# A two-layer encoder trunk on one core: the first norm's factors by a shorter chain, and the first layer's sums queued behind them

## The chip, the cores and the metric

The kernel runs on 1 core of one Trainium2 chip. A core has five engines, each with its own instruction queue that it works through in order: TensorE (PE in the profile, with PEld for its weight loads), VectorE (DVE), ScalarE (ACT), GpSimd (POOL) and SyncE (SP). They wait for each other by semaphores. The metric is the device time of one execution in microseconds, lower is better.

## The reference

The input x has 512 positions of 1024 channels. Two layers follow each other. Each normalizes x, projects it by one wide matrix, runs three branches (a gated linear scan, a spatial gating, a windowed attention), merges them by gates, adds the result to x, and adds a squared-ReLU MLP of a second norm of x. A last norm ends the trunk. What the change touches is the norm and what is computed from it at once:

```python
def rms_norm(x, w):
    xf = x.astype(jnp.float32)
    y = xf * lax.rsqrt(jnp.mean(xf * xf, axis=-1, keepdims=True) + EPS)
    return (y * w.astype(jnp.float32)).astype(x.dtype)
...
for l in range(DEPTH):
    xn = rms_norm(x, ln1[l])
    z = xn @ w_in[l]   # split into the inputs of the branches and their gates
    ...
    x = x + merged @ w_out[l]
    hn = rms_norm(x, ln2[l])
    x = x + jnp.square(jax.nn.relu(hn @ w_up[l])) @ w_down[l]
return rms_norm(x, final_norm)
```

## The kernel before

**The norm's factor is applied late.** The kernel multiplies x by the norm's weights, projects that without waiting for the root, and multiplies each product by the factor of its row, rs = (mean of squares + eps)^-0.5, when it takes the product out of PSUM. So the projections can start before the factors are known, but no product leaves PSUM without them.

**How the factors come about.** For the first layer (`norm_feat`) ScalarE squares the eight pieces of x (four blocks of 128 rows, two halves each) with a running sum of each piece (L286, the tile ss). VectorE adds the halves (L291, tile s), then scales by 1/1024 and adds epsilon (L261, tile ms), and GpSimd raises that to the power -0.5 (L263, tile rs, 128 x 4). Both are traced with high priority. The other norms (`norm_tok`: the second norm of a layer, the first norm of the second layer, and the last norm in `finish`, L1084) go the same way. The norm of the scan's heads also uses `rstd_c`, but has one sum only. Three small operations of VectorE (L721 to L723, tile gsc) make half, minus half and minus one times the factors, for the products that need a sign or a half.

**Exact products in two parts.** Each float32 operand of a product is split: ScalarE rounds it to a high part (L196 for weights, L251 for activations, tiles wh and xs), VectorE subtracts to get the rest (L197 and L252, tiles wl and xs), and TensorE does three products of the parts. There are three tiles each for high and low weights.

**What runs first.** `project_bu` projects one branch's input by four weight chunks (products bu, L201 to L203); `norm_rows` then broadcasts rs over the partitions by TensorE (L270, product bc), ScalarE copies that to SBUF (L338, tile rb), and VectorE takes the four products out with it (L685). Next are three wide blocks of the projection. Each is done by the function `seven`, a scheme that replaces eight block products by seven: it needs sums and differences of the activations' blocks and of the weights' blocks.

- `left_x` makes the activation sums for four pairs of channel blocks (k = 0 to 3): in `left_sums` L369, L371, L372 and L375 (tile sf), then splits (L251, L252).
- `early_sums` makes weight sums in place: t1 = b11 + b12 (L392) and b12 + b22 (L394).
- `seven` makes b11 = t1 + b22 for product 6 (L420) and b21 + b11 for product 4 (L422), and splits each product's weights. The order of the first block is 1, 7, 6, 2, 5, 4, 3. Products 1 and 2 use activations as they are; products 7 and 6 need sums. Product 6 accumulates on the banks of product 1 (tA), which ScalarE must have read out with rs first (L732); product 7 (tC) needs banks that hold bu until L685.

In the profile, t is the first wide block (tA, tB, tC are its banks), g the other two. GELU of bu (L699 to L702) and the norm of the spatial gating (L813 to L819, with a power of one column at L818) are filled in between.

**What sets the order.** No order is written out by hand here. A planner simulates the program while it is built and fixes each engine's queue: it takes operations by priority when their inputs are ready by its own estimate. `high_priority` (and `hp()`, once `boost[0]` is set) raises the priority of what is traced inside. `tc.issue_after(ins)` puts every instruction that is traced in its block on ins's engine behind ins in that engine's queue; nothing else is made to wait.

At the start (L158, L159) one small square on ScalarE and one small power on GpSimd are run on constants.

Of the kernel before, what the change touches and what calls it, by code (L numbers as in the profile page):

```python
# [7 lines left out]
F32R = mybir.dt.float32r  # L8
U8 = mybir.dt.uint8
AF = mybir.ActivationFunctionType  # L10
# [4 lines left out]
D = 1024  # L15
# [44 lines left out]
def trunk(tc, xT, xt, ws, vec, fnb, bsb, snk, wst, rope, cmask, amask, ident, out):  # L60
# [49 lines left out]
    def SM(tag, w):  # L110
        return pad.tile([P, w], F32, tag="sm_" + tag, bufs=4 if tag == "lb" else NSM, name=nm(tag))
# [44 lines left out]
    nc.vector.memset(pad_t, 0.0)  # L156

    nc.scalar.activation(pad_t[:, 1:2], pad_t[:, 0:1], AF.Square)  # L158
    nc.gpsimd.tensor_tensor(pad_t[:, 2:3], onep_t, mhalf_t[:, 0:1], ALU.pow)  # L159

    def ln_ap(which, l, kt):
        c = {"ln1": 0, "ln2": 16, "fn": 32}[which] + (l * 8 if which != "fn" else 0) + kt
# [95 lines left out]
    def rstd_c(pt, n):  # L258
# [4 lines left out]
        nc.gpsimd.tensor_tensor(r, t, mhalf_t[:, 0:w], ALU.pow)  # L263
        return r

    def bcast(c):

        pt = PT("s", "bc")
        for j in range(4):
            nc.tensor.matmul(pt[:, j * P:(j + 1) * P], ap_of(c, j, [[0, P]]), id_t, start=True, stop=True)  # L270
        return pt
# [4 lines left out]
    def norm_feat(l, xf, xrows):  # L276

        n = Norm()
        n.xs, n.xf = [], xf
        for k in range(KT):  # L280
            hi, lo = T("x", "xh", F32R), T("x", "xl", F32R)
            split(xf[k], hi, lo, ln_ap("ln1", l, k))
            n.xs.append((hi, lo))
        ss = SM("ss8", 8)
        for j, x in enumerate(xrows):
            nc.scalar.activation(T("jk", "jk"), x, AF.Square, accum_out=ss[:, j:j + 1])  # L286
        for k in range(KT):
            nc.scalar.activation(xf[k], xf[k], AF.Copy, scale=ln_ap("ln1", l, k))
        s = SM("s4", 4)
        with tc.high_priority():  # L290
            nc.vector.tensor_tensor(s, ap_of(ss, 0, [[2, 4]]), ap_of(ss, 1, [[2, 4]]), ALU.add)  # L291
            n.rc = rstd_c(s, D)
        return n

    def norm_tok(which, l, xr, keep):

        n = Norm()
        n.xs, n.xf = [None] * KT, [None] * KT
        n.ss = SM("ss8", 8)

        def add(t, fl):
            j = T("jk", "jk")
            nc.scalar.activation(j, xr[t][fl], AF.Square, accum_out=n.ss[:, t * 2 + fl:t * 2 + fl + 1])

        def turn(fl, ts, banks="ss"):

            w = len(ts) * P
            c0 = ts[0] * P
            for d in range(4 * fl, 4 * fl + 4):
                if n.xs[d] is None:  # L310
                    n.xs[d] = (T("x", "xh", F32R), T("x", "xl", F32R))
                    if keep:
                        n.xf[d] = T("z" if d < 4 else "l", "xf")
                pt = PT(banks[d % 2], "xT")
                for i, t in enumerate(ts):
                    nc.tensor.transpose(pt[:, i * P:(i + 1) * P], xr[t][fl][:, (d % 4) * P:(d % 4 + 1) * P], id_t)
                src = pt[:, 0:w]
                parts = [x[:, c0:c0 + w] for x in n.xs[d]]
                if keep:
                    xf = n.xf[d][:, c0:c0 + w]  # L320
                    nc.scalar.activation(xf, src, AF.Copy, scale=ln_ap(which, l, d))
                    split(xf, *parts)
                else:
                    split(src, *parts, ln_ap(which, l, d))

        def end():
            s = SM("s4", 4)
            nc.vector.tensor_tensor(s, ap_of(n.ss, 0, [[2, 4]]), ap_of(n.ss, 1, [[2, 4]]), ALU.add)
            n.rc = rstd_c(s, D)

        n.add, n.turn, n.end = add, turn, end
        return n

# [43 lines left out]
        split(sb_.rearrange("p a b -> p (a b)"), *b_)  # L377
        h.update({5: two(a_, 0), 6: two(a_, 1), 7: two(b_, 0), 3: two(b_, 1)})

    def left_x(n):  # L380

        res = []
        for k in range(4):
            h = {1: two(n.xs[k], 0), 2: two(n.xs[k + 4], 0), 4: two(n.xs[k + 4], 1)}
            left_sums(lambda: T("xs", "xs", F32R), h, n.xf[k], n.xf[k + 4])
            res.append(h)
        return res

    def early_sums(raw):
        b11, b12, b22, b21, t1 = raw  # L390
        for i in range(2):
            nc.vector.tensor_tensor(t1[i], b11[i], b12[i], ALU.add)  # L392
        for i in range(2):
            nc.vector.tensor_tensor(b12[i], b12[i], b22[i], ALU.add)  # L394

    def seven(raw, hs, name, on, order=(1, 2, 6, 7, 5, 4, 3), between=None, apart=False):

        b11, t3, b22, b21, t1 = raw
        V = nc.vector

        banks = {}
        use = {1: ("c", b11, "P1"), 2: ("m", b21, "P2"), 6: ("c", b11, "P16"), 7: ("a", t3, "P7"),
               5: ("c", t1, "P165"), 4: ("a", b21, "P74"), 3: ("c", b22, "P1653")}

        def mms(pt, p, k, xh, xl, hi, lo, c, start):
            t = slice(p * P, (p + 1) * P)
            nc.tensor.matmul(pt, xh[:, t], hi[:, c], start=start and k == 0, stop=False, skip_group_check=True)  # L407
            nc.tensor.matmul(pt, xl[:, t], hi[:, c], start=False, stop=False, skip_group_check=True)  # L408
            nc.tensor.matmul(pt, xh[:, t], lo[:, c], start=False, stop=k == 3, skip_group_check=True)  # L409

        for n in order:
            tag, w, which = use[n]
            start = n in (1, 2, 7)
            if start:
                banks[tag] = [PT(tag, name + {"c": "A", "m": "B", "a": "C"}[tag]) for _ in range(2)]
            pts = banks[tag]
            with hp():
                for i in range(2):
                    if n == 6:
                        V.tensor_tensor(b11[i], t1[i], b22[i], ALU.add)  # L420
                    elif n == 4:
                        V.tensor_tensor(b21[i], b21[i], b11[i], ALU.add)  # L422
# [256 lines left out]
    for l in range(DEPTH):  # L679
# [31 lines left out]
        if l == 0:  # L711
            bu = project_bu()

        hx = left_x(n1)
        if l == 0:
            raw = uload(l, "un", 0)
            early_sums(raw)
            boost[0] = True
        rc = n1.rc
        sc = SM("gsc", 12)  # L720
        nc.vector.tensor_scalar(sc[:, 0:4], rc, 0.5, None, ALU.mult)  # L721
        nc.vector.tensor_scalar(sc[:, 4:8], rc, -0.5, None, ALU.mult)
        nc.vector.tensor_scalar(sc[:, 8:12], rc, -1.0, None, ALU.mult)  # L723
        vt = [None] * 4
        bv = [None] * 4

# [45 lines left out]
        for u in range(3):  # L772
            nxt = uload(l, "un", u + 1) if u < 2 else None
            if u == 0:
                seven(raw, hx, "t", on_tok, (1, 7, 6, 2, 5, 4, 3), (lambda: bu.extend(project_bu())) if l else None)
            else:
                seven(raw, hx, "g", on_gate(u - 1))
            if nxt:
                early_sums(nxt)
            raw = nxt  # L780
# [299 lines left out]
        def finish(ts):  # L1080

            n = len(ts)
            ss = SM("s4", 4)[:, 0:n]
            nc.vector.tensor_tensor(ss, ap_of(n1.ss, 2 * ts[0], [[2, n]]), ap_of(n1.ss, 2 * ts[0] + 1, [[2, n]]), ALU.add)  # L1084
            rc = rstd_c(ss, D)
# [185 lines left out]
```

## Time and profile before

| what | value |
|---|---|
| median of 3 runs | 1714.54 us |
| lowest and highest | 1712.42 and 1716.99 us |
| the profiled execution | 1714.73 us |
| its span, first to last instruction | 1712.9 us |
| mean granted TensorE clock | 0.994 |
| instructions | 22985 |
| data moved by DMA | 199.85 MB, mean 117 GB/s |

All rows quoted further down are from the profiled execution. Its times are microseconds from the start of the span. A row of a timeline gives start and duration, engine, line of the kernel, operation, output and inputs by the program's names with their shape, how many such instructions are merged, and in brackets how long the engine had been idle and what ended that. A tile's buffer numbers are left out, so all sums of activations are called sf. The granted clock is the share of TensorE's full speed that the chip allowed in a stretch.

### The profile page before, as it was taken

What the parts mean: (1) busy time and instruction counts of PE and PEld (TensorE: products, weight loads), DVE (VectorE), ACT (ScalarE), POOL (GpSimd) and SP (SyncE); (2) the same over time, 40 slices, a digit from 0 to 9 for tenths busy, and PEclk for the clock granted to TensorE, in tenths of its full rate; (3) what the DMA queues carried; (4) which work ended last, traced back from release to release, by engine and by line L of the source; (5) the groups of instructions that cost most, each with busy time, mean ns of one, the idle gap of its engine ahead of it and who ended that gap; (6) DMA issues with size and microseconds to landing.
All of it is one profiled execution on the core that took longest, in us unless ns stands there. A gap on an engine that the chain in (4) does not pass through costs nothing.

```text
span 1712.9 us, 22985 instructions
## 1 busy us (share of the span) xinstructions
PE 1675.5 (98%) x8536; PEld 1379.8 (81%) x8536; DVE 1285.7 (75%) x2049; ACT 1009.5 (59%) x1691; POOL 122.0 (7%) x198
## 2 busy tenths in 40 slices
PE   7999999999999999999999999999999999999997
PEld 5788887887778888888878888888877788888886
DVE  7896987678465758687889869876875567676877
ACT  6565578677325645455666666877882355545464
POOL 1021000000320000000010210000004100000001
PEclk9999999999999999999999999999999999999999
DMA  8243222231465233332333332322216453232311
GB/s 318 77 148 108 87 87 87 87 105 56 156 237 184 88 122 98 100 111 99 123 123 98 136 106 84 105 87 87 98 44 248 158 185 99 99 112 85 124 61 50
DMA packets 58144, 199.85 MB, mean 117 GB/s; under 512 B 7888, under 2 KB 8144, under 8 KB 58032
## 3 DMA queue, kind: packets, MB, share of 16 engines
q1 hardware_dynamic: 44496, 154.46, 27.0%
q0 software_dynamic: 13248, 43.40, 6.9%
q8 instruction: 67, 1.10, 0.3%
q10 hardware_dynamic: 288, 0.52, 0.1%
q14 instruction: 45, 0.37, 0.1%
HBM read 177.38 MB, written 20.97 MB: 116 GB/s over the span
## 4 chain that ended last, share of the span: by engine, by line
PE 86%; ACT 5%; DVE 4%; DMA 2%; issue 1%; POOL 1%; SPq 0%; POOLq 0%; ACTq 0%; DVEq 0%
PE up L202 7%; PE up L201 7%; PE up L203 7%; PE dA L408 3%; PE dA L407 3%; PE dA L409 3%; PE po L948 2%; PE gA L407 2%; PE wo L244 2%; PE at L540 2%; PE dC L408 2%; PE dC L407 2%; PE dC L409 2%; PE gA L409 2%; PE gA L408 2%; PE wo L243 2%
## 5 line engine op out<-in xcount | busy, mean ns | idle before, releaser
L196 ACT CAST wh<-wq 128x1024 fp32r<-128x1024 f32 x196 | 206.3, 1052 | 213.5 <-PE dA L408 49.2
L196 ACT CAST wh<-wr 128x1024 fp32r<-128x1024 f32 x171 | 179.6, 1050 | 247.5 <-PE up L202 88.7
L197 DVE TENSOR_TENSOR wl<-wr,wh 128x1024 fp32r<-128x1024 f32 x171 | 208.8, 1221 | 154.2 <-ACT wh L196 153.3
L197 DVE TENSOR_TENSOR wl<-wq,wh 128x1024 fp32r<-128x1024 f32 x196 | 239.0, 1221 | 89.0 <-ACT wh L196 87.8
L202 PE MATMUL up<-xl,wh 128*128 128x512 f32 x512 | 199.1, 389 | 0.0
L203 PE MATMUL up<-xh,wl 128*128 128x512 f32 x512 | 199.0, 389 | 0.0
L201 PE MATMUL up<-xh,wh 128*128 128x512 f32 x512 | 198.6, 389 | 0.0
L201 PEld LDWEIGHTS up<-xh,wh 128*128 128x128 f32 x512 | 96.1, 188 | 20.1
L203 PEld LDWEIGHTS up<-xh,wl 128*128 128x128 f32 x512 | 96.1, 188 | 20.0
L202 PEld LDWEIGHTS up<-xl,wh 128*128 128x128 f32 x512 | 96.1, 188 | 19.7
L407 PE MATMUL dA<-wh,sh 128*128 128x512 f32 x256 | 99.7, 390 | 0.0
L408 PE MATMUL dA<-wh,sh 128*128 128x512 f32 x256 | 99.6, 389 | 0.0
L409 PE MATMUL dA<-wl,sh 128*128 128x512 f32 x256 | 92.6, 389 | 0.0
L580 DVE TENSOR_TENSOR ex<-ex 128x512 f32<-128x512 f32 x112 | 74.8, 685 | 4.7 <-ACT kt L556 4.2
L407 PEld LDWEIGHTS dA<-wh,sh 128*128 128x128 f32 x256 | 48.0, 188 | 10.0
L409 PEld LDWEIGHTS dA<-wl,sh 128*128 128x128 f32 x256 | 48.1, 188 | 10.0
L408 PEld LDWEIGHTS dA<-wh,sh 128*128 128x128 f32 x256 | 48.1, 188 | 9.9
L263 POOL TENSOR_TENSOR rs<-ms,mhalf_t 128x4 f32<-128x4 f32 (+2 forms) x15 | 18.5, 1233 | 493.6 <-DVE ms L261 484.3
L554 DVE TENSOR_TENSOR qt<-qt,q 128x512 f32<-128x512 f32 x56 | 38.4, 686 | 18.9 <-ACT qt L553 18.5
L553 ACT ACTIVATE qt<-ex 128x512 f32<-128x512 f32 x56 | 37.7, 674 | 24.5 <-DVE ex L580 19.4
L251 ACT CAST sh<-sf 128x512 fp32r<-128x512 f32 x64 | 39.6, 619 | 19.4 <-DVE sf L372 17.5
L201 PE MATMUL gz<-xh,wh 128*128 128x512 f32 x128 | 50.7, 396 | 0.0
(405 smaller groups left out, 4343.1 us busy)
## 6 DMA issues: line engine op xcount, KB each, us to landing
wr<-in_ws_dram SPq DMA_DIRECT2D x171, 512.0 KB, 3.4
wq<-in_ws_dram SPq DMA_DIRECT2D x112, 512.0 KB, 4.3
thd<-zt POOLq DMA_DIRECT2D x32, 256.0 KB, 2.5
th<-thd POOLq DMA_DIRECT2D x32, 256.0 KB, 3.4
mgd<-mg POOLq DMA_DIRECT2D x16, 256.0 KB, 2.6
mcd<-th POOLq DMA_DIRECT2D x16, 256.0 KB, 3.1
mC<-mcd POOLq DMA_DIRECT2D x16, 256.0 KB, 7.2
mB<-mgd POOLq DMA_DIRECT2D x16, 256.0 KB, 6.6
```

The lines of the kernel that those rows point to most:

```text
L196: nc.scalar.copy(hi, raw)
L197: nc.vector.tensor_tensor(lo, raw, hi.bitcast(F32), ALU.subtract)
L201: nc.tensor.matmul(pt, whi, xhi, start=first, stop=False)
L202: nc.tensor.matmul(pt, whi, xlo, start=False, stop=False)
L203: nc.tensor.matmul(pt, wlo, xhi, start=False, stop=last)
L251: nc.scalar.copy(hi, src)
L407: nc.tensor.matmul(pt, xh[:, t], hi[:, c], start=start and k == 0, stop=False, skip_group_check=True)
L408: nc.tensor.matmul(pt, xl[:, t], hi[:, c], start=False, stop=False, skip_group_check=True)
L409: nc.tensor.matmul(pt, xh[:, t], lo[:, c], start=False, stop=k == 3, skip_group_check=True)
L553: nc.scalar.activation(qt.rearrange(shp, b=nb, h=2), e_q, AF.Exp)
L554: nc.vector.tensor_tensor(qt, qt, q, ALU.mult)
L580: nc.vector.tensor_tensor(o_ap, o_ap, ap_of(ex, i_, [[istep, 2]] + z), ALU.add)
```

## The change

Each square is scaled by 1024^-0.5 before it is squared, so the running sums are already means; one operation (`rstd_d`) adds the two halves and epsilon. All RMS norms of x use it. The warm-up power at the start goes. In each layer the three factor operations are traced ahead of the activation sums and with high priority, and in the first layer the fourth pair's activation sums, the weight sums b12 + b22 and those of `seven`'s first block (L420, L422) are queued on VectorE behind the last of the three.

```diff
-    nc.gpsimd.tensor_tensor(pad_t[:, 2:3], onep_t, mhalf_t[:, 0:1], ALU.pow)
...
+    def rstd_d(ss, t0, w):
+
+        t = SM("ms", 4)[:, 0:w]
+        nc.vector.scalar_tensor_tensor(t, ap_of(ss, 2 * t0, [[2, w]]), EPS, ap_of(ss, 2 * t0 + 1, [[2, w]]), ALU.add, ALU.add)
+        r = SM("rs", 4)[:, 0:w]
+        nc.gpsimd.tensor_tensor(r, t, mhalf_t[:, 0:w], ALU.pow)
+        return r
...
-            nc.scalar.activation(T("jk", "jk"), x, AF.Square, accum_out=ss[:, j:j + 1])
+            nc.scalar.activation(T("jk", "jk"), x, AF.Square, scale=D ** -0.5, accum_out=ss[:, j:j + 1])
...
-        s = SM("s4", 4)
         with tc.high_priority():
-            nc.vector.tensor_tensor(s, ap_of(ss, 0, [[2, 4]]), ap_of(ss, 1, [[2, 4]]), ALU.add)
-            n.rc = rstd_c(s, D)
+            n.rc = rstd_d(ss, 0, 4)
...
+    def behind(mark):
+
+        return tc.issue_after(mark.ins) if mark else contextlib.nullcontext()
+
-    def left_x(n):
+    def left_x(n, mark=None):
...
-            left_sums(lambda: T("xs", "xs", F32R), h, n.xf[k], n.xf[k + 4])
+            with behind(mark if k == 3 else None):
+                left_sums(lambda: T("xs", "xs", F32R), h, n.xf[k], n.xf[k + 4])
...
-    def early_sums(raw):
+    def early_sums(raw, mark=None):
...
-        for i in range(2):
-            nc.vector.tensor_tensor(b12[i], b12[i], b22[i], ALU.add)
+        with behind(mark):
+            for i in range(2):
+                nc.vector.tensor_tensor(b12[i], b12[i], b22[i], ALU.add)
...
-            with hp():
+            with hp(), behind(mark):
                 for i in range(2):
                     if n == 6:
                         V.tensor_tensor(b11[i], t1[i], b22[i], ALU.add)
...
-        hx = left_x(n1)
+        rc = n1.rc
+        sc = SM("gsc", 12)
+        with tc.high_priority():
+            nc.vector.tensor_scalar(sc[:, 0:4], rc, 0.5, None, ALU.mult)
+            nc.vector.tensor_scalar(sc[:, 4:8], rc, -0.5, None, ALU.mult)
+            mark = nc.vector.tensor_scalar(sc[:, 8:12], rc, -1.0, None, ALU.mult)
+        hx = left_x(n1, mark if l == 0 else None)
         if l == 0:
             raw = uload(l, "un", 0)
-            early_sums(raw)
+            early_sums(raw, mark)
             boost[0] = True
-        rc = n1.rc
-        sc = SM("gsc", 12)
-        nc.vector.tensor_scalar(sc[:, 0:4], rc, 0.5, None, ALU.mult)
-        nc.vector.tensor_scalar(sc[:, 4:8], rc, -0.5, None, ALU.mult)
-        nc.vector.tensor_scalar(sc[:, 8:12], rc, -1.0, None, ALU.mult)
...
-                seven(raw, hx, "t", on_tok, (1, 7, 6, 2, 5, 4, 3), (lambda: bu.extend(project_bu())) if l else None)
+                seven(raw, hx, "t", on_tok, (1, 7, 6, 2, 5, 4, 3), (lambda: bu.extend(project_bu())) if l else None, mark=None if l else mark)
```

The squares in `norm_tok` are scaled in the same way, and `end` there and `finish` (L1084) call `rstd_d` in place of the sum and `rstd_c`.

More of the change, by code (lines that the diff above doesn't have):

```diff
@@ L302, in add @@
             j = T("jk", "jk")
-            nc.scalar.activation(j, xr[t][fl], AF.Square, accum_out=n.ss[:, t * 2 + fl:t * 2 + fl + 1])
+            nc.scalar.activation(j, xr[t][fl], AF.Square, scale=D ** -0.5, accum_out=n.ss[:, t * 2 + fl:t * 2 + fl + 1])
         def turn(fl, ts, banks="ss"):
@@ L326, in end @@
         def end():
-            s = SM("s4", 4)
-            nc.vector.tensor_tensor(s, ap_of(n.ss, 0, [[2, 4]]), ap_of(n.ss, 1, [[2, 4]]), ALU.add)
-            n.rc = rstd_c(s, D)
+            n.rc = rstd_d(n.ss, 0, 4)
         n.add, n.turn, n.end = add, turn, end
@@ L392, in early_sums, with seven @@
             nc.vector.tensor_tensor(t1[i], b11[i], b12[i], ALU.add)
-        for i in range(2):
-            nc.vector.tensor_tensor(b12[i], b12[i], b22[i], ALU.add)
-    def seven(raw, hs, name, on, order=(1, 2, 6, 7, 5, 4, 3), between=None, apart=False):
+        with behind(mark):
+            for i in range(2):
+                nc.vector.tensor_tensor(b12[i], b12[i], b22[i], ALU.add)
+    def seven(raw, hs, name, on, order=(1, 2, 6, 7, 5, 4, 3), between=None, apart=False, mark=None):
         b11, t3, b22, b21, t1 = raw
@@ L1082, in finish @@
             n = len(ts)
-            ss = SM("s4", 4)[:, 0:n]
-            nc.vector.tensor_tensor(ss, ap_of(n1.ss, 2 * ts[0], [[2, n]]), ap_of(n1.ss, 2 * ts[0] + 1, [[2, n]]), ALU.add)
-            rc = rstd_c(ss, D)
+            rc = rstd_d(n1.ss, ts[0], n)
             for i, t in enumerate(ts):
```

## The prediction

> **What bounds the kernel now.** I read the page first. TensorE is busy nearly all the time, so only a stretch where it stands still or runs slowly can be worth anything.
>
> ```profile
> PE 1675.5 (98%) x8536; PEld 1379.8 (81%) x8536; DVE 1285.7 (75%) x2049; ACT 1009.5 (59%) x1691; POOL 122.0 (7%) x198
> ```
>
> Then the waits of TensorE alone (engine, line, what it waited for: us in total, times, longest).
>
> ```profile
> PE bu L201 <- ACT wh L251: 5.8, 1, 5.8
> PE bc L270 <- POOL rs L263: 5.2, 1, 5.2
> ```
>
> The first is the start of the program, which the change leaves alone. The second is the longest wait inside it: the broadcast of the first norm's factors (bc) waits for GpSimd's power, rs. The timeline shows how that wait comes about (start, duration, engine, line, operation; the bracket is the idle time before).
>
> ```profile
> 29.05 0.19 ACT L286 ACTIVATION_READ_ACCUMULATOR jk<-xt 128x1 f32 x1
> ...
> 31.90 0.15 DVE L291 TENSOR_TENSOR s<-ss 128x4 f32<-128x4 f32 x1
> 31.97 1.22 DVE L420 TENSOR_TENSOR wq<-wq,wq 128x1024 f32<-128x1024 f32 x1
> 33.11 1.22 DVE L394 TENSOR_TENSOR wq<-wq,wq 128x1024 f32<-128x1024 f32 x1
> ...
> 35.72 1.22 DVE L420 TENSOR_TENSOR wq<-wq,wq 128x1024 f32<-128x1024 f32 x1
> ...
> 36.85 0.16 DVE L261 TENSOR_SCALAR ms<-s 128x4 f32<-128x4 f32 x1
> 36.92 0.41 DVE L372 SCALAR_TENSOR_TENSOR sf<-sf,x 128x256 f32<-128x256 f32 x1
> 37.10 4.89 POOL L263 TENSOR_TENSOR rs<-ms,mhalf_t 128x4 f32<-128x4 f32 x1 [12.53 <-DVE ms L261]
> ...
> 39.86 1.22 DVE L197 TENSOR_TENSOR wl<-wq,wh 128x1024 fp32r<-128x1024 f32 x1
> 42.02 0.17 DVE L721 TENSOR_SCALAR gsc<-rs 128x4 f32<-128x4 f32 x1 [0.94 <-POOL rs L263]
> ```
>
> The squares are complete at 29.24. VectorE adds the halves at 31.90, but the mean and epsilon follow only at 36.85: five sums stand between them in VectorE's queue. Then the power takes 4.89 us. TensorE meanwhile finishes what needs no factors:
>
> ```profile
> 36.43 0.39 PE L409 MATMUL tA<-wl,xh 128*128 128x512 f32 x1
> 42.04 2.08 PE L270 MATMUL bc<-id_t,rs 128*128 128x128 f32 x8 [5.23 <-POOL rs L263]
> 43.77 0.77 PE L407 MATMUL tA<-wh,xs 128*128 128x512 f32 x1
> ```
>
> The table by stretches (busy PE, PEld, DVE, ACT, POOL; then granted clock) gives the price.
>
> ```profile
> 36.85:42.04 5.19, 0.00 (x0) 0.00 (x1) 4.25 (x8) 1.67 (x4) 4.89 (x1) 0.94 0.41 124
> 42.04:48.30 6.26, 6.26 (x19) 5.29 (x20) 4.41 (x11) 2.98 (x5) 0.00 (x0) 0.51 0.16 66
> ```
>
> The hole costs 5.19 us itself, and the granted clock then is 0.51 for 6.26 us, so 6.26 x 0.49 = 3.1 us more. **The stage is worth 8.3 us at most.** The Trainium skill (TensorE: Matmul & The Clock Gate, Part 1) has the array's clock halved after an idle window of about 3.4 us; the 0.51 behind this hole agrees.
>
> **Why the power takes 4.89 us.** Another power of the same size, and some of one column, beside the VectorE operations that ran then:
>
> ```profile
> 872.74 1.03 POOL L263 TENSOR_TENSOR rs<-ms,mhalf_t 128x4 f32<-128x4 f32 x1
> 108.70 0.55 POOL L818 TENSOR_TENSOR lr<-lr,mhalf_t 128x1 f32<-128x1 f32 x1 [3.72 <-DVE lr L817]
> ```
>
> ```profile
> 953.90 0.68 DVE L702 SCALAR_TENSOR_TENSOR bv<-gs,bv 128x512 f32<-128x512 f32 x1
> 954.07 0.93 POOL L818 TENSOR_TENSOR lr<-lr,mhalf_t 128x1 f32<-128x1 f32 x1 [4.73 <-DVE lr L817]
> 120.44 4.66 POOL L818 TENSOR_TENSOR lr<-lr,mhalf_t 128x1 f32<-128x1 f32 x1
> 123.46 1.21 DVE L420 TENSOR_TENSOR wq<-wq,wq 128x1024 f32<-128x1024 f32 x1
> ```
>
> The one at 954.07 ends at 955.00, 0.42 after L702 ends (954.58); the one at 120.44 ends at 125.10, 0.43 after a row of sums ends (124.67). The disputed one ends at 41.99, 0.91 after L197 ends at 41.08. So a power stands still while VectorE reads two tensors of SBUF without a pause, and needs 0.4 us (one column) or 0.9 us (four) after that. The Trainium skill (SBUF — State Buffer, Who interferes with whom) says that a VectorE instruction with two SBUF inputs contends with a GpSimd instruction that reads SBUF, and that the loser waits until the first finishes. By that the power would be through behind one operation (37.33 plus 0.91, at 38.2); the trace has it wait for all five, and I go by the trace.
>
> **The change, part by part.**
>
> *One operation for mean and epsilon.* The place of s at 31.90 is taken by ms itself, at 0.17 us (what L721 takes). The power can start at about 32.25, the 0.25 being what lies between ms and the power at 36.85 and 37.10. Scale in the squares is an operand of the same instruction: nothing, bounds 0 and 8 x 0.19 us on ScalarE (one more readout each, like that at 29.05), ahead of five idle microseconds there (the cast at 34.41 below). The other norms lose one small step each; only the last is on the path:
>
> ```profile
> 1705.74 0.16 DVE L1084 TENSOR_TENSOR s<-ss 128x1 f32<-128x1 f32 x1 [0.56 <-ACT jk L303]
> 1705.94 0.15 DVE L261 TENSOR_SCALAR ms<-s 128x1 f32<-128x1 f32 x1
> ```
>
> There 1705.94 - 1705.74 = 0.2 us goes from the end.
>
> *Sums queued behind the factors.*
>
> ```profile
> 34.41 1.06 ACT L196 CAST wh<-wq 128x1024 fp32r<-128x1024 f32 x1 [5.17 <-DVE wq L394]
> ```
>
> ```profile
> 47.77 0.42 DVE L369 TENSOR_TENSOR sf<-x 128x256 f32<-128x256 f32 x1
> 48.11 0.68 DVE L700 SCALAR_TENSOR_TENSOR gs<-gs,bu 128x512 f32<-128x512 f32 x1
> ...
> 55.97 1.22 DVE L422 TENSOR_TENSOR wq<-wq,wq 128x1024 f32<-128x1024 f32 x1
> ```
>
> Four weight sums (two L394, two L420; 1.14 us apart in a row, 4.56 us) and the fourth pair's activation sums, which ran only from 47.77 on anyway, now stand behind the last of the three factor operations (L721 to L723). Not queued so are the third pair's sums (L371, L372, L375: 3 x 0.42 us, like L369 above); they are ready at 32 and may hold the power up. So rs comes between 33.3 (no hold: 32.25 + 1.03) and 35 (hold by those and a split); I take 34.2: the three end at about 33.3, plus 0.91. The three factor operations, 0.07 us apart, end at 34.4. VectorE loses about 1.2 us standing before them. Behind them in its queue are the weight sums, for which ScalarE's casts wait, and for those TensorE.
>
> *TensorE.* It has work until 36.82, so with rs at 34.2 the broadcast neither waits nor makes a hole. What is late next is the first product from sums (its evacuations of tA need rs, its weights an L420, a cast of 1.06 and a split of 1.22). First L420 from 34.4 to 35.6, cast to 36.7: in time for TensorE's 36.85 + 0.9 for bc at full clock (1.73 from 42.04 to the next product, halved).
>
> *VectorE's backlog.* This decides how much of 8.3 us remains.
>
> ```profile
> 42.04:62.97 20.93, 20.43 (x81) 16.66 (x81) 17.05 (x27) 13.19 (x20) 0.00 (x0) 0.85 0.17 55
> 62.97:120.00 57.03, 56.83 (x254) 46.53 (x255) 54.81 (x70) 36.04 (x48) 5.51 (x10) 1.00 0.44 144
> ...
> 128.00:171.00 43.00, 43.00 (x194) 35.71 (x193) 27.95 (x31) 23.60 (x29) 4.87 (x9) 1.00 0.30 107
> ```
>
> From 36.85 to 62.97, where three products and the broadcast are done, VectorE works 4.25 + 17.05 = 21.3 us. Some 3 us of that is GELU (five operations like L700 at 48.11), which nothing awaits then. Left are 18.3, plus the 4.56 moved in, less the 1.26 of the third pair that now runs before: 21.6 us, from 34.4 to 56.0 without a pause. It paused for 26.1 - 21.3 = 4.8 us, of which 0.94 (L721) and 6.26 - 4.41 = 1.85 (between 42.04 and 48.30, for the broadcast of rs) fall away: 2 us of pauses stay, and 58.0 is the late end. But two L422, a split and an evacuation in that stretch (some 4.3 us) serve products that come after the three; without them it is 53.7. TensorE by itself would be through at 36.85 + 0.9 + 72 matmuls x 0.224 (56.83 over 254) = 53.9. I take the middle between 53.9 and 58.0 and half a microsecond for waits on casts: 62.97 becomes 56.5, **6.5 us gained**. Bounds: 53.9 (9.0 gained) and 59 (4 gained: pauses as now, rs at 36). The GELU operations put off find room: from 128 to 171 VectorE works 27.95 of 43.
>
> *The factor operations put ahead, with priority.* 3 x 0.07 us of VectorE on its way; the second layer's likewise. VectorE's pauses hide them; without that cover they cost 0.2.
>
> *The warm-up power removed.*
>
> ```profile
> 1.05 0.56 POOL L159 TENSOR_TENSOR pad_t<-onep_t,mhalf_t 128x1 f32<-128x1 f32 x1 [0.61 <-DVE pad_t L156]
> ```
>
> The first power of all took 0.56, what a later one of one column takes (0.55): I see no price of a first use that it pays, so removing it costs 0. The bound above is 3.86, 4.89 less 1.03, if the excess of the real one were a first use after all. A rule speaks against this edit: the Trainium skill (GPSIMD Engine Reference, 2.1 Instruction dispatch) gives about 6 us for the first call of a freshly loaded kernel, with nothing visible in the profile. No run here shows it; by that figure 0.7 us of the sum would be left.
>
> *DMA.* The loads of the next weights (L186 on SP's queue) are released by products, so they move with them; their share is 0.16 to 0.17 there and hides.
>
> Sum: 6.5 + 0.2 = 6.7 us. The profiled execution took 1714.73 (span 1712.9 and 1.8 around it), 0.2 above the median of the runs, 1714.54; from the median, 1714.54 - 6.7 = **1707.8 us**.
>
> **Rivals.**
>
> *The power stays long.* Either it is starved by unmarked work behind ms (splits of 1.22, more activation sums) or pays a first use: 32.25 + 4.89 = 37.1. Then bc ends at 38.1, the first L420 at 38.6, its cast at 39.7, against the product at 43.77 before: 4 us. Against it: the 4.66 at 120.44 ends with VectorE's row, far from a first use. For it: I can't see how many splits the order puts there. 1710.5.
>
> *It does not do what it says.* The planner orders by its own estimate of times; it may put other work into the place freed, so that ms or the first products come as late as now, or lose the gain in smaller holes later. Then only the 0.2 at the end is left: 1714.3.
>
> *VectorE becomes the bound up to 120 us: slower.* From 31.90 to 120 it works 4.95 (all of 31.90 to 36.85) + 4.25 + 17.05 + 54.81 = 81.1 us; with 1.2 for the power and the 7.0 it paused from 36.85 on, that ends at 121.2. If nothing could be put off beyond 120, TensorE would be 1.2 us later than now, and with a hole that halves the clock once more (3.1) some 4.3: 1719. It decides from the point where put-off GELU and norm work is due before 128; the 15 us free behind speak against.
>
> **How the numbers follow.** The forecast (4 to 9.0 us gained and 0.2, 1705.3 to 1710.3) has 0.60; the long power 0.20; no effect 0.12; slower 0.08. A measurement of this kernel can tell about 0.3%, 5.1 us, from no change, so the bound is 1709.4. Faster by more: 0.53 of the forecast and 0.05 of the long power, 0.58. Slower by more, above 1719.7: 0.03 of the slower case and 0.03 for holes elsewhere, 0.06. The rest, 0.36, is within. The range leaves out the slower case and the upper half of no effect, and below reaches 1704.3, 1 us under the bound for the order of later work.
>
> **What would show it.** Right: ms near 31.9 and no s; the power about 1 to 2 us long, ended by 34 to 35; L394 and L420 behind L723; no TensorE wait for rs, no 0.5 clock before 60; small waits of TensorE for wh or wl of that stage instead. Wrong: a power near 4.9 us with VectorE idle beside it (a first use), or with splits beside it (starved); a hole over 3 us at 37 with the clock halved; the first product later than 39.

## The result, and the profile after

The changed kernel took **1728.16 us** (median of 5 runs, 1726.94 to 1729.93) against 1714.54 us before (1712.42 to 1716.99): the ratio of after to before is 1.0082, 95% interval [1.0069, 1.0094]. The change makes the kernel slower, by some 14 us, where 1707.8 us was forecast. The median lies far above the range's upper end of 1714.0, and above the 1719 of the slower rival.

The stage that the prediction worked on went nearly as forecast. In the changed kernel the lines are renumbered: L268 is the one operation for mean and epsilon, L270 the power, L277 bc, L403 and L429 the weight sums (before L394 and L420), L195 and L196 cast and split of the weights, L416 to L418 the products (before L407 to L409), L726 to L728 the three factor operations, L742 the read-out of tA. Its timeline (columns as in the prediction):

```profile
32.20 0.16 DVE L268 SCALAR_TENSOR_TENSOR ms<-ss 128x4 f32<-128x4 f32 x1
...
32.45 1.15 POOL L270 TENSOR_TENSOR rs<-ms,mhalf_t 128x4 f32<-128x4 f32 x1 [7.57 <-DVE ms L268]
...
33.64 0.17 DVE L726 TENSOR_SCALAR gsc<-rs 128x4 f32<-128x4 f32 x1
...
33.86 2.35 DVE L429 TENSOR_TENSOR wq<-wq,wq 128x1024 f32<-128x1024 f32 x2
...
36.13 2.35 DVE L403 TENSOR_TENSOR wq<-wq,wq 128x1024 f32<-128x1024 f32 x2
...
36.53 1.31 ACT L742 ACTIVATE vt<-tA,rs 128x512 f32<-128x512 f32 x2 [2.20 <-PE tA L418]
...
36.95 1.05 PE L277 MATMUL bc<-id_t,rs 128*128 128x128 f32 x8
37.74 1.04 ACT L195 CAST wh<-wq 128x1024 fp32r<-128x1024 f32 x1
...
39.15 2.00 ACT L195 CAST wh<-wq 128x1024 fp32r<-128x1024 f32 x2
...
41.20 0.56 PE L416 MATMUL tA<-wh,xs 128*128 128x512 f32 x1 [3.20 <-ACT wh L195]
```

The power takes 1.15 us instead of 4.89 and is done at 33.60; the broadcast no longer waits. TensorE waits once, 3.2 us, for the first weights made of sums. The table over the prediction's two stretches (us; busy PE, PEld, DVE, ACT, POOL; granted clock):

```profile
36.85:42.04 5.19, 1.99 (x13) 1.61 (x12) 5.19 (x8) 4.89 (x7) 0.00 (x0) 0.95 0.09 17
42.04:62.97 20.93, 20.93 (x86) 16.71 (x85) 19.80 (x26) 12.77 (x19) 0.00 (x0) 0.93 0.38 125
```

The hole is 5.19 - 1.99 = 3.2 us where it was 5.19; behind it the clock costs 20.93 x 0.07 = 1.5 us where it cost 20.93 x 0.15 = 3.1. That is 3.6 us better. The first products of the second wide block, gA, mark the end of the stage (the answer for one tile, first of before and then of after; behind "x8:" are shortest, median and longest duration in ns, then first and last start in us):

```profile
L407 PE MATMUL gA<-wh,xh x8: 389/389/499, 79.7 to 85.5; 128*128 128x512 f32 x8
```

```profile
L416 PE MATMUL gA<-wh,xh x8: 389/390/496, 76.5 to 82.3; 128*128 128x512 f32 x8
```

So at 80 us the changed kernel is **3.2 us ahead**, and at the end of the span (1728.0 against 1712.9) 15.1 us behind: 18 us are lost somewhere else. The first lines of the page say on which engine (before's is in the prediction):

```profile
PE 1692.5 (98%) x8536; PEld 1381.7 (80%) x8536; DVE 1288.0 (75%) x2042; ACT 1008.0 (58%) x1691; POOL 120.2 (7%) x197
```

TensorE is busy 17.0 us longer with the same 8536 products. It does not wait more; its products take longer. The view of costliest groups (line, operation, tiles, shapes, count; busy us and mean ns of one) tells which. Before, then after:

```profile
L202 PE MATMUL up<-xl,wh 128*128 128x512 f32 x512 | 199.1, 389 | 0.0
L203 PE MATMUL up<-xh,wl 128*128 128x512 f32 x512 | 199.0, 389 | 0.0
L201 PE MATMUL up<-xh,wh 128*128 128x512 f32 x512 | 198.6, 389 | 0.0
L407 PE MATMUL dA<-wh,sh 128*128 128x512 f32 x256 | 99.7, 390 | 0.0
L408 PE MATMUL dA<-wh,sh 128*128 128x512 f32 x256 | 99.6, 389 | 0.0
L409 PE MATMUL dA<-wl,sh 128*128 128x512 f32 x256 | 92.6, 389 | 0.0
```

```profile
L201 PE MATMUL up<-xl,wh 128*128 128x512 f32 x512 | 199.4, 390 | 0.0
L202 PE MATMUL up<-xh,wl 128*128 128x512 f32 x512 | 199.3, 390 | 0.0
L200 PE MATMUL up<-xh,wh 128*128 128x512 f32 x512 | 198.9, 390 | 0.0
L417 PE MATMUL dA<-wh,sh 128*128 128x512 f32 x256 | 101.7, 397 | 0.0
L416 PE MATMUL dA<-wh,sh 128*128 128x512 f32 x256 | 100.9, 394 | 0.0
L418 PE MATMUL dA<-wl,sh 128*128 128x512 f32 x256 | 93.7, 394 | 0.0
```

The products of the MLP's first half (up) are as they were; those of its second half (dA) are longer. Products overlap, so their cost is seen best in a stretch of nothing else. In the first layer's MLP the 192 products of one up block, and then the 168 of one down block (dA, dB, dC) with the start of the next, take, before and after:

```profile
614.89:658.41 43.52, 43.52 (x193) 36.04 (x192) 28.23 (x42) 23.86 (x38) 0.00 (x0) 1.00 0.25 85
658.41:696.49 38.08, 38.08 (x169) 31.53 (x168) 30.06 (x35) 17.52 (x19) 0.00 (x0) 1.00 0.39 125
```

```profile
616.34:659.87 43.53, 43.53 (x193) 36.07 (x192) 28.24 (x42) 23.83 (x38) 0.00 (x0) 1.00 0.26 85
659.87:698.99 39.12, 39.12 (x169) 31.56 (x168) 30.30 (x35) 17.46 (x20) 0.00 (x0) 1.00 0.37 122
```

No stretch has a wait, both have full clock. The down block is 1.04 us longer: 1.04 / 168 = 6.2 ns for each product, 227 ns from one start to the next before and 233 after. The up block takes the same to 0.01 us. Over the whole trace, the starts of consecutive products of 128x512 lie 227.3 ns apart before. After, 2610 of them, in 23 groups (all of dA, dB, dC, wo, yB and yC, and of tA, tC, gA, gC those that use xs), lie 233.1 ns apart, and the other 3593 lie 227.7 apart. The first make 2610 x 5.8 = 15.1 us, the others 1.4.

What these 23 groups have in common is not in the diff but in the addresses that the compiled programs give. The three buffers of the tile s, 32 bytes each, are no longer allocated: `SM("s4", 4)` was their only use. All that is allocated behind them moves by 96 bytes towards the start of SBUF: xs from 183296 to 183200, wq from 138240 to 138144, and sh in part, mgh, mgl and part of yh and yl. The weights' parts wh (42496) and wl (54784) and the activations xh and xl (83456) lie ahead and stay. In before all these addresses are multiples of 512. Each slow group multiplies a tile that moved with wh or wl, which didn't; up and yA, whose tiles all stayed, are unchanged. It holds product by product too. With each record of after set against its instruction in the program, 3813 products whose streamed operand lies a multiple of 256 bytes from both its own weights and the next product's (which are loaded meanwhile) have the next start 227.8 ns behind their own on the mean; for 2211 whose two offsets are both 96 or 160 modulo 256 it is 233.5. Traffic of other engines with moved tiles doesn't explain it: the products of the wide blocks with xh and xl, beside casts of the moved wq, have 228.6 ns on the mean, and those of wo, beside casts of wr, which stayed, 233.6.

### The profile page after: what moved, and what is told of

It is laid out like the page before. It is cut to its first block, busy times and chain, and to the rows that moved or that the text cites. A ratio compares the mean times of both kernels' runs of the same rounds, so it can differ in the third digit from the quotient of the medians.

```text
span 1728.0 us, 22972 instructions
## 1 busy us (share of the span) xinstructions
PE 1692.5 (98%) x8536; PEld 1381.7 (80%) x8536; DVE 1288.0 (75%) x2042; ACT 1008.0 (58%) x1691; POOL 120.2 (7%) x197
## 4 chain that ended last, share of the span: by engine, by line
PE 85%; ACT 5%; DVE 4%; issue 3%; DMA 2%; POOL 0%; SPq 0%; POOLq 0%; ACTq 0%; DVEq 0%
PE up L201 7%; PE up L200 7%; PE up L202 7%; PE dA L417 3%; PE dA L416 3%; PE dA L418 3%; PE po L958 2%; PE wo L243 2%; PE wo L242 2%; PE dC L417 2%; PE wo L244 2%; PE dC L418 2%; PE dC L416 2%; PE at L549 2%; PE gz L200 1%
## 5 line engine op out<-in xcount | busy, mean ns | idle before, releaser
L195 ACT CAST wh<-wq 128x1024 fp32r<-128x1024 f32 x196 | 205.2, 1048 | 217.1 <-PE dA L417 54.6
L196 DVE TENSOR_TENSOR wl<-wr,wh 128x1024 fp32r<-128x1024 f32 x171 | 209.1, 1223 | 158.3 <-ACT wh L195 157.4
L195 ACT CAST wh<-wr 128x1024 fp32r<-128x1024 f32 x171 | 179.4, 1049 | 249.4 <-PE up L201 89.3
L196 DVE TENSOR_TENSOR wl<-wq,wh 128x1024 fp32r<-128x1024 f32 x196 | 239.0, 1222 | 92.6 <-ACT wh L195 91.4
L416 PE MATMUL dA<-wh,sh 128*128 128x512 f32 x256 | 100.9, 394 | 0.0
L418 PE MATMUL dA<-wl,sh 128*128 128x512 f32 x256 | 93.7, 394 | 0.0
L416 PEld LDWEIGHTS dA<-wh,sh 128*128 128x128 f32 x256 | 48.1, 188 | 11.8
L418 PEld LDWEIGHTS dA<-wl,sh 128*128 128x128 f32 x256 | 48.1, 188 | 11.3
L243 PE MATMUL wo<-wh,mgl 128*128 128x512 f32 x128 | 51.4, 401 | 0.0
L244 PE MATMUL wo<-wl,mgh 128*128 128x512 f32 x128 | 51.3, 403 | 0.0
```

Source lines behind the costliest of these rows:

```text
L195: nc.scalar.copy(hi, raw)
L196: nc.vector.tensor_tensor(lo, raw, hi.bitcast(F32), ALU.subtract)
L243: nc.tensor.matmul(pts[t], xl, hi[:, c], start=False, stop=False)
L244: nc.tensor.matmul(pts[t], xh, lo[:, c], start=False, stop=k == nk - 1)
```

## The experiments

**Theory (place).** The loss comes from where the operands of a product lie, and the edits themselves gain some 4 us. **Rival 1 (order).** The new order of the sums, or the lost warm-up, brings other traffic beside the products, and the addresses are a coincidence. Within the theory, what counts may be an operand's own address (at 32, 64 or more bytes) or the place of the two against each other. Ratios are against runs of the kernel before on the same chip, with 95% intervals.

### The room given back, and the kernel before moved

The changed kernel with 96 bytes put back by widening an unused tile that lies ahead of s's place:

```diff
-    pad_t = pad.tile([P, 16], F32, name="pad_t")
+    pad_t = pad.tile([P, 40], F32, name="pad_t")
```

> The changed kernel with one constant tile made 96 bytes wider, so that every tile behind it lies where it lay before the change; nothing else differs. Theory (place): the tile s is gone, its three buffers of 32 bytes with it, and all that is allocated behind it moved by 96 bytes, so that products that read a moved tile stand 233 ns apart instead of 227. Then the products with sh, xs and mgh come back to 227 ns, the time falls by about 16 us to 1711 or 1712, and what is left of the change is a gain of about 3 us. Rival (order): the planner's new order of the queues makes TensorE slower; then the time stays at 1728 and the spacing at 233.

Measured: 1711.15 us (1710.39 to 1713.69) against 1714.98; ratio 0.998 [0.9971, 0.9989]. Products with moved tiles: 227.3 ns, and the down block is back at 38.08 us:

```profile
654.58:692.66 38.08, 38.08 (x169) 31.53 (x168) 30.05 (x35) 17.53 (x19) 0.00 (x0) 1.00 0.38 125
```

Beside the width of the one memset that fills the tile, each engine's queue holds the same instructions in the same order as in the changed kernel; the 24 columns are worth 17 us. The reverse, with the kernel before and 32 bytes more (24 columns), and with 64 (32 columns):

> The kernel before with the same tile 32 bytes wider, which moves the tiles behind it by 32 bytes; order and instructions as before. Theory (place): the products with sh, xs and mgh go to 233 ns and the time to about 1731. Rival (order): 1714.5, as before.

> The kernel before with the tile 64 bytes wider. Theory (place), if the boundary that counts is 64 bytes: 1714.5 and 227 ns. If it is 128 bytes or more: about 1731 and 233 ns, like a move by 32. Rival (order): 1714.5.

Measured: 1730.66 us (1728.93 to 1732.18), 1.0089 [1.0075, 1.0103]; and 1730.73 us (1728.39 to 1732.68), 1.0089 [1.0075, 1.0103]. Both are as slow as the change, with none of it in them: each engine's queue holds before's instructions in before's order. Rival 1 falls. In the 32-byte kernel the up and down blocks that were shown above are, and below them the down block of the 64-byte kernel:

```profile
618.96:662.48 43.52, 43.52 (x193) 36.04 (x192) 28.23 (x42) 23.74 (x38) 0.00 (x0) 1.00 0.25 85
662.48:701.49 39.01, 39.01 (x169) 31.55 (x168) 30.27 (x35) 17.49 (x19) 0.00 (x0) 1.00 0.37 122
```

```profile
661.04:700.12 39.08, 39.08 (x169) 31.57 (x168) 30.28 (x35) 17.46 (x19) 0.00 (x0) 1.00 0.37 122
```

The 64-byte kernel shows that a boundary of 64 bytes isn't what counts. Next, everything moved by 32 bytes together, by a small tile ahead of all operands in the kernel before:

```diff
+    gap_t = cst.tile([P, 8], F32, name="gap_t")
+    nc.vector.memset(gap_t, 0.0)
```

> The kernel before with a tile of 32 bytes ahead of all others, so that every operand of every product is moved by 32 bytes, the weights wh and wl and the activations xh and xl too. Theory (place), if only the loaded operand (the stationary one) counts or only one price is paid: all 6300 wide products at 233 ns, 6300 x 6 ns = 38 us more, 1752. If the streamed operand costs the same again: 239 ns and about 1790. Rival (order): 1714.5.

Measured: 1716.22 us (1713.35 to 1718.22), 1.0005 [0.9996, 1.0015]. Both numbers that I had put on it, 1752 and 1790, are far off: I had thought of each operand's own address, so moving all of them should have cost more. (1714.5 was Rival 1's number, but Rival 1 had it for the moves by 32 and 64 bytes too.) No operand of the wide products lies on a multiple of 512 here, or even of 64, and none is slow:

```profile
612.83:656.35 43.52, 43.52 (x193) 36.05 (x192) 28.22 (x42) 23.85 (x38) 0.00 (x0) 1.00 0.25 85
656.35:694.43 38.08, 38.08 (x169) 31.54 (x168) 30.05 (x35) 17.52 (x19) 0.00 (x0) 1.00 0.38 125
```

So my reading by own addresses falls, and what counts is the **place of a product's two operands against each other**.

### How far apart

The kernel before with pad_t at 48 columns (128 bytes more) and at 80 (256 more):

> The kernel before, with the small unused tile pad_t widened from 16 to 48 columns: every tile allocated behind it lies 128 bytes further on, tiles ahead of it stay. It tells what step of the relative place of a product's two operands costs time: 32 and 64 bytes cost 16 us (233 instead of 227 ns for products that use a moved tile with an unmoved one). If the place counts modulo 128 bytes or less: 1714.5 and 227 ns. If it counts modulo 256 or 512 bytes: 1730.7 and 233 ns.

> The kernel before, with pad_t widened to 80 columns: tiles behind it lie 256 bytes further on. If the place counts modulo 256 bytes or less: 1714.5 and 227 ns for products of a moved with an unmoved tile; if it counts modulo 512: 1730.7 and 233 ns.

Measured: 1727.8 us (1726.41 to 1730.34), 1.0081 [1.0062, 1.0099], and 1713.55 us (1712.51 to 1717.0), 0.9996 [0.9987, 1.0005]. The down block of each:

```profile
660.99:699.90 38.91, 38.91 (x169) 31.63 (x168) 30.27 (x35) 17.47 (x19) 0.00 (x0) 1.00 0.37 122
```

```profile
657.57:695.64 38.07, 38.07 (x169) 31.54 (x168) 30.05 (x35) 17.55 (x19) 0.00 (x0) 1.00 0.38 125
```

128 bytes cost, 256 are free: of the three answers, modulo 256 is the one left. All eight kernels in one table (the offset is that of the moved tiles against the unmoved, beside before's; the spacing is that of the 23 groups):

| kernel | offset, bytes | spacing, ns | median, us |
|---|---|---|---|
| before | 0 | 227.3 | 1714.54 |
| all moved by 32 | 0 | 227.3 | 1716.22 |
| before and 256 | 256 | 227.3 | 1713.55 |
| before and 32 | 32 | 232.7 | 1730.66 |
| before and 64 | 64 | 232.8 | 1730.73 |
| before and 128 | 128 | 232.1 | 1727.8 |
| after | -96 | 233.1 | 1728.16 |
| after, room back | 0 | 227.3 | 1711.15 |

### The parts of the change, at before's addresses

With the room back the change itself gains 3.8 us. Which part? First without the queueing (no marks; the shorter norm and the early factor operations stay):

```diff
-        hx = left_x(n1, mark if l == 0 else None)
+        hx = left_x(n1)
...
-            early_sums(raw, mark)
+            early_sums(raw)
...
-                seven(raw, hx, "t", on_tok, (1, 7, 6, 2, 5, 4, 3), (lambda: bu.extend(project_bu())) if l else None, mark=None if l else mark)
+                seven(raw, hx, "t", on_tok, (1, 7, 6, 2, 5, 4, 3), (lambda: bu.extend(project_bu())) if l else None, mark=None)
```

> The changed kernel with the 96 bytes put back, and without the queueing: no sum is put behind the factors any more; the one operation for mean and epsilon and the early factor operations stay. VectorE then has five operations in a row behind ms, 4 x 1.14 + 0.34 us. Theory (starved): the power of 32.4 ends 0.9 us after that row, at about 38.1, so it lasts 5 to 6 us, and TensorE waits for rs from 37 on for 1 to 1.5 us; but the casts are ready sooner, the first product from sums comes at about 41, as with the queueing, and the time is 1710 to 1712. Rival (the 4.89 us were a first use or the late ms alone): the power lasts 1.0 to 1.2 us as with the queueing, TensorE waits for nothing, 1708 or less.

Measured: 1710.55 us (1708.32 to 1712.15), 0.9973 [0.9963, 0.9984]. Its timeline:

```profile
31.84 0.15 DVE L268 SCALAR_TENSOR_TENSOR ms<-ss 128x4 f32<-128x4 f32 x1
31.91 1.22 DVE L429 TENSOR_TENSOR wq<-wq,wq 128x1024 f32<-128x1024 f32 x1
32.08 5.69 POOL L270 TENSOR_TENSOR rs<-ms,mhalf_t 128x4 f32<-128x4 f32 x1 [7.57 <-DVE ms L268]
...
35.65 1.21 DVE L429 TENSOR_TENSOR wq<-wq,wq 128x1024 f32<-128x1024 f32 x1
37.80 0.17 DVE L726 TENSOR_SCALAR gsc<-rs 128x4 f32<-128x4 f32 x1 [0.94 <-POOL rs L270]
```

With the sums free to run, a row of five stands beside the power again, and it takes 5.69 us; it ends at 37.77, 0.91 after the row's end at 36.86. That is the starvation that the prediction read off, made again. Yet no time is lost: TensorE waits 1.1 us for rs and 1.4 for a cast in place of 3.2 for a cast, since the sums that ran meanwhile let the casts start early. Then the queueing alone, with the norm's factors made the long way (s, then ms; s is back, so its room too):

```diff
-            nc.scalar.activation(T("jk", "jk"), x, AF.Square, scale=D ** -0.5, accum_out=ss[:, j:j + 1])
+            nc.scalar.activation(T("jk", "jk"), x, AF.Square, accum_out=ss[:, j:j + 1])
...
-            n.rc = rstd_d(ss, 0, 4)
+            s = SM("s4", 4)
+            nc.vector.tensor_tensor(s, ap_of(ss, 0, [[2, 4]]), ap_of(ss, 1, [[2, 4]]), ALU.add)
+            n.rc = rstd_c(s, D)
```

> The kernel with the queueing and the early factor operations, but the first norm in its old form (plain squares, a sum, then mean and epsilon in a second operation); the tile s is there again and with it the old place of everything behind. Theory: the sums that stood between s and ms are behind the factors now, so ms comes about 0.5 us after s; power 1 to 1.5 us, rs by 34.5, far ahead of TensorE, which needs it at 37: the same time as with both, 1711 to 1712. Rival (the short chain is what gains): nearer to 1714.

Measured: 1711.95 us (1710.19 to 1714.41), 0.9984 [0.9975, 0.9993]; the power starts at 32.79, takes 1.20 us, and TensorE waits 3.6 us for the cast. So either half of the change gives what both give, within the intervals. They don't add up: in all three kernels TensorE ends up waiting for the same thing, the cast that product 6 needs (1.4, 3.6 and 3.2 us).

### The casts' order

In the timeline after, ScalarE stands 2.20 us until tA can be read out (L742 at 36.53), though L429's first sum is done by 35.1; then come, by the program's queue, both casts for product 7 (37.74 and the first of the pair at 39.15) and only then product 6's, for which the product at 41.20 waits. Product 6 moved ahead of product 7 in the first block of each layer (the line serves both), all else as with the room back:

```diff
-                seven(raw, hx, "t", on_tok, (1, 7, 6, 2, 5, 4, 3), (lambda: bu.extend(project_bu())) if l else None, mark=None if l else mark)
+                seven(raw, hx, "t", on_tok, (1, 6, 7, 2, 5, 4, 3), (lambda: bu.extend(project_bu())) if l else None, mark=None if l else mark)
```

> The changed kernel with the 96 bytes put back, and the first block's products in the order 1, 6, 7, 2, 5, 4, 3 in place of 1, 7, 6, 2, 5, 4, 3. In the changed kernel TensorE waits 3.2 us for the cast of product 6, which stands in ScalarE's queue behind two read-outs of product 1 and both casts of product 7. Theory (the hole moved into ScalarE's queue): with product 6 cast first TensorE goes on at 38 to 39, has no hole over 1.5 us and no half clock there; 3 to 5 us less than with the old order, 1706 to 1708. Rival (VectorE's backlog sets the stage): the hole comes back a little later, 1711.

Measured: **1707.75 us** (1707.52 to 1709.15), 0.9963 [0.995, 0.9975], ahead of both kernels. A cast now starts before the read-outs, and the first product of sums comes at 37.45:

```profile
34.82 1.06 ACT L195 CAST wh<-wq 128x1024 fp32r<-128x1024 f32 x1 [0.83 <-DVE wq L429]
...
37.45 0.48 PE L416 MATMUL tA<-wh,xs 128*128 128x512 f32 x1
```

In the waits of TensorE (30 to 84 us) the 3.2 is gone; two short ones took its place:

```profile
PE tA L418 <- DVE wl L196: 1.0, 1, 1.0
PE tA L416 <- ACT vt L742: 0.6, 1, 0.6
```

The time fell within the expected 1706 to 1708, but not all of it for the expected reason. The half clock came here too: it was 0.50 for 3.41 us from 40.74 on. And the first product of gA starts at 74.3 where it was 75.4 with the room back, so only 1.1 us of the lead lies in this stage. By the end of the profiled spans (1705.7 and 1709.5) it is 3.8. About 1.0 of the rest comes near 430 us, where the clock was halved for 3.41 us instead of 6.83, and 0.7 between 850 and 905 us, where the second layer's first block stands; the remaining 1.0 is not tied to a cause.

The same order without the marks:

> Product 6 first, the 96 bytes put back, and no queueing. Theory: the power is starved until about 38.1, but the cast of product 6 is done by then; TensorE waits 1.2 us for rs and again some tenths, the clock stays up, and the time is 1 to 2 us above that with queueing and product 6 first: 1707 to 1709. Rival (queueing is worth nothing once the casts are in order): the same within 0.5 us; or less, if VectorE's pause for the power costs more than the wait for rs.

Measured: 1709.11 us (1708.6 to 1710.66), 0.9968 [0.9957, 0.9979]. I had expected a starved power again; it took 1.04 us. VectorE happened to stand still for its first half, until 33.42, waiting for a load:

```profile
32.88 1.04 POOL L270 TENSOR_TENSOR rs<-ms,mhalf_t 128x4 f32<-128x4 f32 x1 [7.72 <-DVE ms L268]
33.42 1.23 DVE L429 TENSOR_TENSOR wq<-wq,wq 128x1024 f32<-128x1024 f32 x1 [0.63 <-DMA wq<-in_ws_dram]
```

TensorE waits 2.2 us for bu instead: L694 has its rb at 40.90, but its turn in VectorE's queue comes only at 42.59, behind splits and sums. The clock was not halved there (1.00 from 36 to 48 us). So the time just above the expected 1707 to 1709 says nothing for the theory. The intervals overlap, so the marks are worth 1.4 us at most with this order, and that is not settled. Last, the warm-up power put back into the fastest kernel:

```diff
+    nc.gpsimd.tensor_tensor(pad_t[:, 2:3], onep_t, mhalf_t[:, 0:1], ALU.pow)
```

> The room-back kernel with the sixth product taken before the seventh (1707.75), with the warm-up power at the start of the program put back. If the power of the first norm pays no first use, as the 1.2 us of it without any warm-up says: 1707.8 again, within 1 us, and the power stays at 1.2 us. If removing the warm-up cost something that another place hides (a first use, the load of code): the first power becomes shorter by up to 0.7 us and the time 0.5 to 1 us lower.

Measured: 1708.9 us (1707.29 to 1710.67), 0.9962 [0.9949, 0.9975], the same as without it by ratio. The first norm's power takes 1.16 us with the warm-up and 1.15 without. No cost of the removal is to be seen.

## Why the prediction was wrong

- **The step that failed: the sum had no term for the removed tile.** I costed each instruction that the change removes, adds or moves, and never the room that s had taken. It measured 17.0 us (1728.16 against 1711.15 with the room back), more than twice all that I worked out, and with the other sign. The products of a moved with an unmoved tile went from 227.3 to 233.1 ns apart. No rival held it: the slower one had VectorE as the bound, and VectorE is not. Nothing in the profile of before pointed there, since all the spacings were 227 ns; the diff did, by a tile's last use that goes.
- **The size of the gain: 3.8 us with the room back, forecast 6.7.** The step "First L420 from 34.4 to 35.6, cast to 36.7: in time" is the term that was off. The sum came even 0.5 us earlier than forecast (L429 from 33.86). The casts did not: the one awaited ended at 41.15, since I took ScalarE as free and it had two read-outs of tA and product 7's casts ahead in its queue. The hole stays at 3.2 us with half of the clock's loss. With the casts' order changed the kernel takes 1707.75. That this equals the forecast is no merit of it: it is another kernel, and most of its further gain lies outside the stage. The working was also at odds with itself: the upper bound of 9.0 us gained is more than the 8.3 that it gave the stage at most.
- **Right:** no wait for rs, rs at 33.60 within 33.3 to 35, the four sums behind L728. ms came at 32.20, where 31.90 was worked out. The 34.2 taken for rs let the third pair's three sums hold the power up; they did run beside it, from 32.28 to 33.63, but it ended 0.90 us past the first of them (32.70) and not past the last. That a row of VectorE's operations without a pause holds the power up until 0.9 us past the row's end was shown by the kernel without queueing.
- **Its own signs:** two that it had named for being wrong came: a hole over 3 us with the clock halved (3.20 us, up to 41.20; then a clock of 0.50 for 3.41 us from 41.51 on, which is the 0.93 over 42.04 to 62.97) and a first product of sums later than 39 (41.20). Of the signs for being right, no 0.5 clock before 60 and only small waits for wh failed with them.
- **The long power** did come, in the kernel without queueing: 1710.55 us, the rival's 1710.5. That the times agree is luck: the rival let the weight sums start only behind the factors, and here they ran before them. Nor is the long power a loss against the short one: with its casts done early that kernel is as fast as the one with both parts (0.9973 [0.9963, 0.9984] and 0.998 [0.9971, 0.9989]).
- **VectorE's backlog** was not the bound up to 63 us: TensorE is busy for all of 20.93 us there, with VectorE at 19.80.
- **The end of the program:** one operation instead of two, as said. From the start of the last squares' readout to the power it is 1705.52 to 1706.23 before, 0.71, and 1720.74 to 1721.26 after, 0.52:

```profile
1720.74 0.19 ACT L308 ACTIVATION_READ_ACCUMULATOR jk<-xr 128x1 f32 x1
...
1720.95 0.16 DVE L268 SCALAR_TENSOR_TENSOR ms<-ss 128x1 f32<-128x1 f32 x1 [0.77 <-ACT jk L308]
...
1721.26 0.94 POOL L270 TENSOR_TENSOR rs<-ms,mhalf_t 128x1 f32<-128x1 f32 x1 [0.35 <-DVE ms L268]
```

```profile
1705.52 0.19 ACT L303 ACTIVATION_READ_ACCUMULATOR jk<-xr 128x1 f32 x1
...
1706.23 0.93 POOL L263 TENSOR_TENSOR rs<-ms,mhalf_t 128x1 f32<-128x1 f32 x1 [0.33 <-DVE ms L261]
```

- **Where the 18.5 us went** that lie between the profiled spans of the changed kernel and the one with the room back (1728.0 - 1709.5): both traces hold the same 8536 products in the same order, so each distance from one start to the next can be set against the other's. The 2610 distances behind products of the 23 groups make 15.4 us, the other short ones 1.6, and those over 0.3 us in either trace 1.5, most of it at 1335 us: there the changed kernel's clock was halved once more, and the other's was not. Without that, 15.4 + 1.6 = 17.0 us is what the medians differ by.

```profile
1335.16:1338.58 3.42, 3.42 (x11) 2.59 (x10) 3.14 (x6) 1.41 (x3) 2.91 (x7) 0.50 1.02 412
```

## What to carry to other kernels

Before an edit that adds or drops a buffer is priced by its instructions, look where it moves what is allocated behind it; here a dropped tile of 96 bytes cost 17 us, and 24 unused columns took them back. When a kernel is slower than its waits explain, compare the mean duration of the same product, group by group: an even 2% on some groups and none on others came from their operands here, not from the schedule. And when an operation is made earlier, follow its consumer to that consumer's own queue: the sum was in time and the cast wasn't.

## What the runs showed of the hardware

- **The place of two operands against each other sets a product's rate.** Offsets of 32, 64, 128 and -96 bytes, beside a base where all of wh, wl, xh, xs, sh and mgh lie on multiples of 512, cost 5 to 6 ns of 227 for each 128x512 product; 0 and 256 cost nothing, and neither does moving both operands by 32. The weight loads' own duration did not show it (188 ns for up, which wasn't slowed, and for dA, which was). The Trainium skill (SBUF — State Buffer, Operand start alignment) lets an operand start at any multiple of its element size and says of its runs that they timed nothing; these runs time it. The Trainium skill (SBUF — State Buffer, Who interferes with whom) has TensorE read weights and the streamed operand by two independent ports and lets only VectorE and GpSimd contend. The rows here speak for something that the two reads share; no run shows what. Which of them waits stays open too. In each kernel 86 products have their streamed operand off against the next product's weights alone, and 86 or 87 against their own alone. The two sorts take 234.6 and 229.3 ns in the changed kernel, 234.5 and 231.8 with 32 bytes, 229.4 and 232.3 with 64, 232.6 and 233.0 with 128: neither is the slower one throughout.

```profile
L416 PEld LDWEIGHTS dA<-wh,sh 128*128 128x128 f32 x256 | 48.1, 188 | 11.8
...
L200 PEld LDWEIGHTS up<-xh,wh 128*128 128x128 f32 x512 | 96.2, 188 | 20.0
```

- **A power that starts beside a row without pauses waits for the whole row.** It took 5.69 us beside five VectorE operations that follow each other without a gap, and ended 0.91 us past the last. Where three sums stood 0.03 and 0.04 us apart beside it, in the changed kernel, it took 1.15 us and ended 0.90 past the first alone; with the queueing alone, likewise 0.91 past the one that was running when it started (L377 of that kernel, until 33.08). Where VectorE stood still at its start it took 1.04, though a sum ran beside its second half. These are lengths of the same 128x4 in the same place. That the short gaps let it through is how I read them; no run varied a gap by itself.
- **The length of a wait alone does not fix what the clock loses.** Behind the same hole of 5.2 us the clock was halved for 6.83 us in the kernel before and with 32 bytes, and for 3.41 us with 64 and 128 bytes. Behind two waits of 1.0 and 0.6 us (product 6 first) it was 3.41 us, and behind waits of 0.6 and 2.2 us (the same without the marks) none. So the 3.1 us that the prediction set down for the clock could by these traces have been about half of that.
